# Where the weights lie in their slot, and which half of a k tile comes first: a hybrid RWKV-7 and short convolution block on one core

## The chip, the cores and the metric

The kernel runs on one core of one Trainium2 chip. The metric is the device time of one execution in microseconds (us). Before the change it is 1021.4 us, the median of 3 runs (1020.84 to 1022.16).

## The reference, cut to what matters

One layer over 528 tokens (16 learned ones and 512 of the input), 2048 wide, in float32:

```python
hn = _rmsnorm(h_res, norm_in_g[l])
P = hn @ w_in[l]                       # 2048 -> 65 * 128 columns
Pr, Pc = P[..., :RW_COLS], P[..., RW_COLS:]
prev = jnp.pad(Pr[:, :-1], ((0, 0), (1, 0), (0, 0)))
Pr = Pr + (prev - Pr) * mu_shift[l]
# Pr: r, k, v, g_r (1024 columns each) and two low rank inputs (64 each)
# y = RWKV-7 recurrence of r, decay, k, v, kk, a; 16 heads of 64
y_a = (yn + bonus.reshape(bsz, L, D_RWKV)) * jax.nn.silu(g_r)
# Pc: Bg, Cg, hc, g_c (1024 columns each)
y_b = Bg * _causal_depthwise_conv(Cg * hc, conv_w[l]) * jax.nn.silu(g_c)
h_res = h_res + jnp.concatenate([y_a, y_b], axis=-1) @ w_out[l]
out = _rmsnorm(h_res, norm_f_g)[:, N_META:]
```

What counts here is the first product, `hn @ w_in`: 65 tiles of 128 columns each, which take most of the kernel's time. Everything else is fitted between its matmuls.

## The kernel before, in words

**The projection.** The normalised input lies transposed in SBUF as two parts, xh (the rounded float32r values) and xl (what is left), each of 16 rows (`KT`) of 640 columns (`XROW`, L50), of which 528 are tokens. A tile of the projection is 128 of w_in's columns. Its 2048 by 128 weights come as two transfers of 128 by 1024 (`wr`, three buffers) on SP's queue; each is cut into two quarters of 512 columns, and a quarter is split by ScalarE (the high part, L137) and VectorE or GpSimd (the low part, L138) into a slot `w`. There are six slots in a ring, each 1152 columns wide (`SLOT`) and so 4608 bytes from the next; the high part starts at column `at` of the slot, the low part 512 columns behind it (`slot`, L125). `column` (L115) gives `at` for each tile: 16 for k, v and the low rank inputs (lora), 0 for B and gc, and 8i, 8i + 64, 8i, 8i + 64 for r, g, C, h of index i = 0 to 7. Nothing else depends on `at`. These four lines give 16 different positions.

**The matmuls of a tile** (`steps`, L322, and `main`, L339). A tile is computed for all tokens in one or two pieces, each in its PSUM bank: k, v and lora in pieces of 256 and 272 columns (`FULL`), r, g, C and h in 256 and 258 (`TAIL`), B and gc in one of 512 (`REAL`). Per quarter the pieces come one after the other, the 256 columns first; in a piece the four weight blocks k, and for each block three matmuls: high weights with xh, high weights with xl, low weights with xh. Each matmul has its own weight load. So a tile in two pieces is 4 x 2 x 4 x 3 = 96 matmuls, a quarter 24, a piece of a quarter 12.

```python
for k in ks:
    for n, (ww, xx) in enumerate(((hi, xh), (hi, xl), (lo, xh))):
        nc.tensor.matmul(ps[r], ww[:, w], xx[:, kt, a:b], ...)
```

The change's words count a "distance" from weights to moving columns in bytes, modulo 512.

**Order.** `plan` (L102) lists the tiles: lora, k 0, r 0, B 0 (these four run together over quarters in `mains`, L483), then v 0, k 1, r 1, v 1, g 0, g 1, C 0, h 0, gc 0, and for each further pair of heads k, r, v, k, r, v, g, g, C, h, B, gc; at last C, h, B, gc of 4 to 7. The order of TensorE is written by hand: the projection is a generator of single matmuls, and the other parts of the work call `fill(ns)`, which lets so much of the projection (0.43 ns a column) run between their own matmuls. VectorE, ScalarE, GpSimd and SP are ordered by a scheduler that goes by priorities and expected times, so their order can move when TensorE's does.

**What runs between.** For each pair of heads `prepare` (L628) makes the decay (matmuls tz, ta), the gram matrices (g) and, on VectorE alone, the inverse of small blocks: the blocks go by DMA to sg and come back as d, the result y goes out to sx and comes back as xT. `invert` (L832) then needs xT transposed on VectorE (xn, L845) for the matmuls t (L854). `recur` (L941) runs the recurrence over 9 chunks among the last C, h, B and gc tiles. The finished tiles are read from PSUM by VectorE (`scaled`, L348, line 354 of the profile), in pieces: 256 columns, then the second piece in one or more parts (three for the 272 of k and v). h's result hh goes through GpSimd and ScalarE into cv on VectorE. After the last tile comes the product with w_out (line 1242).

Of the kernel before, what the change touches and what calls it, by code (L numbers as in the profile page):

```python
# [77 lines left out]
def hymba_kernel(ctx: ExitStack, tc: tile.TileContext, xt, xtok, front, w_in, w_out, pv, lup, cst, msk, gf, out):  # L78
# [23 lines left out]
    plan = [("lora", 0), ("k", 0), ("r", 0), ("B", 0), ("v", 0), ("k", 1), ("r", 1), ("v", 1), ("g", 0), ("g", 1)]  # L102
# [10 lines left out]
    N_IN = len(stream)  # L113

    def column(j):  # L115
        what, i = plan[j]
        return {
            "k": 16, "v": 16, "lora": 16, "B": 0, "gc": 0,
            "r": 8 * i, "g": 8 * i + 64, "C": 8 * i, "h": 8 * i + 64,
        }[what]  # L120
    stream += [w_out[0, g] for g in range(3)]
    quarters, chain, low = {}, {}, {}
    state = {"next": 0}
# [5 lines left out]
    def slot_of(q):  # L129
        if q >= 2 * N_IN:  # L130
            return slot(f"w{q}", OUT_AT)
        n = q // 2
        return slot(f"w{q}", column(n % 4 if n < 8 else n // 2))
# [7 lines left out]
    def prefetch(upto):  # L141
        while state["next"] < min(upto, len(stream) if chain else N_IN):
            j = state["next"]
            raw = chain[j - N_IN] if j >= N_IN else wp.tile([P, 1024], F32, tag="raw", name=f"wr{j}", bufs=3)
            state["dma"] = nc.sync.dma_start(raw, stream[j]).ins
            with tc.high_priority(offset=WEIGHTS):
                for q in range(2):
                    split_w(2 * j + q, raw[:, q * 512 : (q + 1) * 512], nc.gpsimd if q and 10 < j < N_IN else nc.vector)
            state["next"] = j + 1
# [172 lines left out]
    def steps(ps, ranges, k4, q, ks=range(4), rs_=range(2)):  # L322
        hi, lo = quarters[q]
        for r, (a, b) in enumerate(ranges):
            if r not in rs_:
                continue
            for k in ks:
                kt = 4 * k4 + k
                w = slice(k * P, (k + 1) * P)
                for n, (ww, xx) in enumerate(((hi, xh), (hi, xl), (lo, xh))):  # L330
                    nc.tensor.matmul(  # L331
                        ps[r], ww[:, w], xx[:, kt, a:b], start=(kt == 0 and n == 0), stop=(kt == KT - 1 and n == 2)
                    )
                    yield (b - a) * 0.43

    def banks(ranges, name, pool, tag):
        return [pool.tile([P, b - a], F32, tag=tag, name=f"ps_{name}_{r}") for r, (a, b) in enumerate(ranges)]

    def main(j, ranges, name):  # L339
        prefetch(2 * j + 4)  # L340
        ps = banks(ranges, name, pm, "main")
        for k4 in range(4):
            if k4 == 1:
                prefetch(2 * j + 5)
            yield from steps(ps, ranges, k4, 4 * j + k4)
        return ps

    def scaled(ranges, ps, dst, base):  # L348
# [134 lines left out]
    def mains():  # L483
# [35 lines left out]
        for j in range(4, len(plan)):  # L519
            what, i = plan[j]  # L520
            rg = FULL if what in ("k", "v") else REAL if what in ("B", "gc") else TAIL
            ps = yield from main(j, rg, f"{what}{i}")
            if what == "B" and i < 4:
                state["split"] = low[4 * j + 4]
            use(what, i, ps)
# [692 lines left out]
    def here(t, n):  # L1218
        return xa[t][:, n * 512 : (n + 1) * 512] if n < 2 else xb[n - 2][:, t]
# [147 lines left out]
    for u, unit in enumerate(units):  # L1367
        half, prod, g = unit
# [53 lines left out]
    with tc.manual_schedule(engines={mybir.EngineType.DVE, mybir.EngineType.Activation, mybir.EngineType.Pool}):  # L1422
# [16 lines left out]
        for part in range(2):  # L1439
# [7 lines left out]
            h = here(1, 2)[:, cols]  # L1447
# [71 lines left out]
```

## Time and profile before

| | |
|---|---|
| median of 3 runs | 1021.4 us |
| the profiled execution | 1022.35 us |
| its span, first to last instruction | 1020.6 us |
| granted TensorE clock, mean over the span | 0.995 |
| tiles of C, h, r, g, k, v (96 matmuls each) without interruption | 11.3 to 11.6 us |
| tiles of B and gc (48 matmuls each) without interruption | 10.9 to 11.4 us |

The page of the profile gives busy time by engine, the chain of work that ended last, and groups of instructions by line; PE is TensorE's matmuls, PEld its weight loads, which overlap them, DVE VectorE, ACT ScalarE, POOL GpSimd, and SP the queue of most DMAs. The view of stretches gives the busy time and number of instructions of each engine between two times. Where its limits are the first matmul of a tile and the first of the next, its length is the time of that tile; an instruction that reaches over a limit is counted too, so the number of matmuls is one or two above 96 there.

### The profile page before, as it was taken

How to read it: one execution, taken by the hardware profiler on the slowest of the kernel's cores; microseconds unless marked ns; L12 is line 12 of the kernel's file. 1: busy time of each engine (PE TensorE's matmuls, PEld its weight loads, DVE VectorE, ACT ScalarE, POOL GpSimd, SP SyncE). 2: the span in 40 equal slices, each digit the busy share in tenths (PEclk: the TensorE clock that was granted, in tenths of full speed). 3: DMA queues.
4: the chain of work that ended last, by engine and by line, in shares of the span. 5: the costliest groups of instructions: out<-in, count | busy, mean ns of one | idle time of the engine just before them, and what ended most of it. 6: DMA issues, size and time to landing. Idle time of an engine off the chain costs nothing.

```text
span 1020.6 us, 23761 instructions
## 1 busy us (share of the span) xinstructions
PE 1001.5 (98%) x9723; PEld 919.9 (90%) x9723; DVE 688.1 (67%) x1305; ACT 393.9 (39%) x729; POOL 274.8 (27%) x292
## 2 busy tenths in 40 slices
PE   9999999999999999999999999999999999999996
PEld 8899998999988999998999998989888897787885
DVE  6677964587765569655568654244555697998787
ACT  7553422344323433322434322222222335545453
POOL 0122323233222323222323222123332333005001
PEclk9999999999999999999999999999999999999999
DMA  9525476446574364864263855977673687695754
GB/s 317 163 69 146 124 197 161 124 119 150 132 191 128 99 165 99 205 179 117 85 167 98 219 141 168 339 248 233 212 215 95 177 270 190 179 321 139 177 127 165
DMA packets 185037, 174.83 MB, mean 171 GB/s; under 512 B 121568, under 2 KB 142816, under 8 KB 184416
## 3 DMA queue, kind: packets, MB, share of 16 engines
q1 hardware_dynamic: 182336, 164.40, 55.0%
q0 software_dynamic: 2304, 8.39, 4.8%
q8 instruction: 76, 1.25, 0.5%
q10 hardware_dynamic: 288, 0.52, 0.1%
q14 instruction: 33, 0.27, 0.1%
HBM read 136.92 MB, written 36.35 MB: 170 GB/s over the span
## 4 chain that ended last, share of the span: by engine, by line
PE 56%; DVE 8%; DMA 3%; issue 3%; ACT 1%; POOL 0%; DVEq 0%; ACTq 0%; SPq 0%; POOLq 0%
PE ps_gc L331 8%; PE ps_B L331 7%; PE ps_h L331 7%; PE ps_C L331 7%; PE ps_v L331 5%; PE ps_g L331 5%; PE ps_k L331 5%; PE ps_r L331 4%; DVE o L1215 3%; DMA wo<-in_w_out_dram 2%; PE M L1242 2%; PE zs L1007 1%; PE zy L1011 1%; PE rz L955 1%; PE g L682 1%
## 5 line engine op out<-in xcount | busy, mean ns | idle before, releaser
L137 ACT CAST w<-wr 128x512 fp32r<-128x512 f32 x252 | 152.8, 618 | 295.4 <-PE ps_k L331 45.0
L138 POOL TENSOR_TENSOR w<-wr,w 128x512 fp32r<-128x512 f32 x119 | 165.4, 1390 | 368.7 <-ACT w L137 317.1
L138 DVE TENSOR_TENSOR w<-wr,w 128x512 fp32r<-128x512 f32 x133 | 96.3, 730 | 105.7 <-ACT w L137 95.7
L331 PE MATMUL ps_k<-xh,w 128*128 128x256 f32 (+1 forms) x512 | 95.9, 284 | 1.1 <-DVE w L138 1.1
L331 PE MATMUL ps_r<-xh,w 128*128 128x256 f32 (+1 forms) x512 | 95.9, 282 | 0.0
L331 PE MATMUL ps_h<-xh,w 128*128 128x258 f32 (+1 forms) x512 | 95.3, 284 | 0.0
L331 PE MATMUL ps_v<-xh,w 128*128 128x272 f32 (+1 forms) x512 | 95.1, 283 | 0.0
L331 PE MATMUL ps_C<-xh,w 128*128 128x258 f32 (+1 forms) x512 | 94.4, 283 | 0.0
L331 PE MATMUL ps_g<-xh,w 128*128 128x258 f32 (+1 forms) x512 | 93.1, 282 | 0.0
L331 PE MATMUL ps_B<-xh,w 128*128 128x512 f32 x256 | 84.3, 398 | 0.0
L331 PEld LDWEIGHTS ps_k<-xh,w 128*128 128x128 f32 x512 | 80.4, 189 | 1.8 <-DVE w L138 1.4
L331 PE MATMUL ps_gc<-xh,w 128*128 128x512 f32 x256 | 81.6, 393 | 0.2 <-DVE w L138 0.2
L331 PEld LDWEIGHTS ps_r<-xh,w 128*128 128x128 f32 x512 | 80.4, 189 | 0.3
L331 PEld LDWEIGHTS ps_h<-xh,w 128*128 128x128 f32 x512 | 80.0, 189 | 0.7
L331 PEld LDWEIGHTS ps_C<-xh,w 128*128 128x128 f32 x512 | 79.9, 189 | 0.6
L331 PEld LDWEIGHTS ps_v<-xh,w 128*128 128x128 f32 x512 | 80.0, 189 | 0.3
L331 PEld LDWEIGHTS ps_g<-xh,w 128*128 128x128 f32 x512 | 79.5, 189 | 0.3
L331 PE MATMUL ps_h<-xl,w 128*128 128x256 f32 (+1 forms) x256 | 72.2, 282 | 0.8 <-issue 0.8
L331 PE MATMUL ps_k<-xl,w 128*128 128x256 f32 (+1 forms) x256 | 72.6, 284 | 0.0
L331 PE MATMUL ps_g<-xl,w 128*128 128x256 f32 (+1 forms) x256 | 72.5, 283 | 0.0
L331 PE MATMUL ps_v<-xl,w 128*128 128x256 f32 (+1 forms) x256 | 72.5, 283 | 0.0
L331 PE MATMUL ps_r<-xl,w 128*128 128x256 f32 (+1 forms) x256 | 72.2, 282 | 0.0
(321 smaller groups left out, 2283.2 us busy)
## 6 DMA issues: line engine op xcount, KB each, us to landing
wr<-in_w_in_dram SPq DMA_DIRECT2D x126, 512.0 KB
ct<-opd SPq DMA_DIRECT2D x64, 288.0 KB
wo<-in_w_out_dram SPq DMA_DIRECT2D x24, 512.0 KB
x<-in_w_out_dram POOLq DMA_DIRECT2D x16, 512.0 KB, 5.7
opd<-ar SPq DMA_DIRECT2D x8, 576.0 KB
opd<-gt SPq DMA_DIRECT2D x16, 288.0 KB
opd<-bt SPq DMA_DIRECT2D x64, 64.0 KB
x<-in_w_out_dram SPq DMA_DIRECT2D x8, 512.0 KB
```

The lines of the kernel that those rows point to most:

```text
L137: nc.scalar.copy(hi, rq)
L138: low[q] = eng.tensor_tensor(out=lo, in0=rq, in1=hi.bitcast(F32), op=ALU.subtract).ins
L331: nc.tensor.matmul(ps[r], ww[:, w], xx[:, kt, a:b], start=(kt == 0 and n == 0), stop=(kt == KT - 1 and n == 2))
L682: nc.tensor.matmul(z[h][:, c - c0], bk[hs, c, h : h + 2, :].rearrange("p a s -> p (a s)"), ar[hs, c].rearrange("p a s -> p (a s)"), start= ...
L955: nc.tensor.matmul(z[e][ho if e else hs, 0, k], t[hs, o : o + CH], t[hs, O_V : O_V + CH] if part else st[hs, 4 * e + k], start=(part == 0 ...
L1007: nc.tensor.matmul(d[hs, j], w, x[hs], start=(a == 0), stop=(a == b - 1))
L1011: nc.tensor.matmul(d[ho, j], t[hs, o : o + CH], x[hs], start=(a == 0), stop=(a == b - 1))
L1215: nc.vector.tensor_tensor(out=lo, in0=rq, in1=hi.bitcast(F32), op=ALU.subtract)
L1242: nc.tensor.matmul(bank[s], left(prod, jj, m, s), w, start=(jj == 0 and n == 0), stop=(jj == 7 and n == 2))
```

## The change

`column` gives one position to k, r, C and lora (16, the default) and one to v, g and h (80), in place of 16 for k, v and lora and of the positions by index for r, g, C and h; B and gc stay at 0. And in the tiles of k that `main` computes (k 1 to k 7) the piece of 272 columns comes before the piece of 256 in each quarter. The number of instructions and the sizes of all buffers stay.

```diff
     def column(j):
-        what, i = plan[j]
-        return {
-            "k": 16, "v": 16, "lora": 16, "B": 0, "gc": 0,
-            "r": 8 * i, "g": 8 * i + 64, "C": 8 * i, "h": 8 * i + 64,
-        }[what]
+        what = plan[j][0]
+        return {"B": 0, "gc": 0, "v": 80, "g": 80, "h": 80}.get(what, 16)
...
         for k4 in range(4):
             if k4 == 1:
                 prefetch(2 * j + 5)
-            yield from steps(ps, ranges, k4, 4 * j + k4)
+            for r in (1, 0) if name[0] == "k" else range(len(ranges)):
+                yield from steps(ps, ranges, k4, 4 * j + k4, rs_=(r,))
         return ps
```

In the scheduler's order of the changed kernel VectorE reads the 272 column piece of k first and the 256 column piece last. A few other instructions change places: in the second pair of heads one transfer `wr` stands ahead of the load of d (d<-sg) on SP's queue, and opd<-ar ahead of the loads of xT; the order around xn there stays.

## The prediction

> **What bounds the kernel now.** I read the page first, then the busy time by stage, then TensorE's list of waits. The span, the busy row and the chain's shares:
>
> ```profile
> span 1020.6 us, 23761 instructions
> PE 1001.5 (98%) x9723; PEld 919.9 (90%) x9723; DVE 688.1 (67%) x1305; ACT 393.9 (39%) x729; POOL 274.8 (27%) x292
> PE 56%; DVE 8%; DMA 3%; issue 3%; ACT 1%; POOL 0%; DVEq 0%; ACTq 0%; SPq 0%; POOLq 0%
> ```
>
> TensorE is busy 98% of the span. The table of stretches says where it isn't (columns: stretch, its length, then busy time and count of PE, PEld, DVE, ACT, POOL, then granted clock, DMA share, GB/s):
>
> ```profile
> 0.00:55.00 55.00, 51.65 (x352) 46.69 (x353) 38.58 (x84) 33.45 (x66) 5.10 (x21) 1.00 0.67 226
> 55.00:329.00 274.00, 270.48 (x2593) 258.41 (x2592) 191.97 (x407) 100.49 (x188) 78.18 (x93) 0.99 0.53 141
> 329.00:479.00 150.00, 150.00 (x1411) 143.47 (x1411) 95.72 (x206) 53.65 (x98) 45.83 (x50) 1.00 0.56 146
> 479.00:629.00 150.00, 150.00 (x1413) 143.51 (x1412) 95.69 (x205) 53.49 (x97) 45.82 (x42) 1.00 0.53 140
> 629.00:853.00 224.00, 223.19 (x3267) 200.24 (x3267) 122.09 (x199) 65.09 (x123) 71.35 (x56) 1.00 0.72 224
> ```
>
> All the tiles of r, C, k, g, h and v but the first k and r lie between 55 and 853 us, and there TensorE rests 274.00 - 270.48 + 224.00 - 223.19 = 4.3 us of 798. So in these stages the end moves with the time that the matmuls themselves take, unless one of the few waits grows. The two longest there are:
>
> ```profile
> engine line waited for: us in total, times, longest us
> PE t L854 <- DVE xn L845: 2.2, 1, 2.2
> PE ps_k L331 <- DVE w L138: 1.1, 1, 1.1
> ```
>
> **The matmuls by distance.** A slot of weights is 4608 bytes apart from the next, a row of the moving x 2560, a weight block 512, and a piece of x starts at byte 0 or 1024: all multiples of 512. So within a tile the distance of weights to moving columns, taken modulo 512 bytes, is one number, 4 x column + 384 (column 16 gives 448, column 80 gives 704 - 512 = 192, as the change has it). Before, r and C of index i stand at 384 + 32i, g and h at 128 + 32i. That makes the old kernel a measurement of its own: equal tiles of 96 matmuls at all 16 distances. Stretches from the first matmul of a tile to the first of the next, where nothing else lies between, give the price of each: C 0, C 1, C 2, C 3, C 4, g 5, C 7 in the first fence (distances 384, 416, 448, 480, 0, 288, 96).
>
> ```profile
> 134.22:145.75 11.54, 11.54 (x98) 11.54 (x97) 5.11 (x20) 3.11 (x5) 2.71 (x4) 1.00 0.86 219
> 275.47:286.92 11.45, 11.45 (x98) 11.45 (x97) 9.46 (x34) 3.11 (x5) 2.71 (x3) 1.00 1.03 282
> 430.19:441.46 11.27, 11.27 (x98) 11.27 (x97) 10.48 (x31) 3.16 (x5) 3.75 (x2) 1.00 0.64 180
> 579.97:591.41 11.44, 11.44 (x98) 11.44 (x97) 10.65 (x31) 3.15 (x5) 3.68 (x2) 1.00 0.61 171
> 629.06:640.61 11.55, 11.55 (x97) 11.55 (x96) 4.41 (x6) 3.12 (x5) 2.59 (x2) 1.00 0.84 276
> 418.69:430.19 11.50, 11.50 (x98) 11.50 (x97) 4.99 (x15) 3.63 (x6) 2.69 (x4) 1.00 0.91 219
> 808.19:819.55 11.36, 11.36 (x97) 11.36 (x96) 10.57 (x16) 5.14 (x10) 2.82 (x2) 1.00 0.78 223
> ```
>
> And h 0 and h 1 (128 and 160):
>
> ```profile
> 145.75:157.30 11.55, 11.55 (x98) 11.55 (x97) 7.65 (x24) 1.15 (x2) 1.30 (x1) 1.00 0.91 233
> 286.92:298.37 11.44, 11.44 (x98) 11.44 (x97) 6.92 (x11) 1.25 (x2) 1.29 (x1) 1.00 0.67 169
> ```
>
> Two things are to be seen. A tile at 448 takes 11.27 us, the others 11.36 to 11.55, though PEld is busy in every one from end to end. And h agrees with C to 0.01 us at a distance 256 higher, so 192 should be worth what 448 is. It isn't the other engines: DVE is busier beside C 2 (10.48 us) than beside C 0 (5.11), and DMA share 1.03 beside C 1 goes with a shorter tile than 0.86 beside C 0.
>
> The Trainium skill speaks against this change. "TensorE: Matmul & The Clock Gate", section "Step-by-step: what each phase is for", says that the moving operand and the weight load have independent SBUF read ports, so that loading the next weights takes nothing from the running matmul; by that rule no column would matter and the time would stay 1021.4 us. The rows above do not agree with it: 0.28 us of 11.55 hang on the column.
>
> **r, C, g and h, term by term.** No instruction is added or removed; a slot is 1152 columns wide whatever column is used. Against 11.27 each index saves: 0: 11.54 - 11.27 = 0.27; 1: 0.18; 2: 0; 3: 0.17; 4: 0.28; 5: 0.23; 7: 0.09. Index 6 (64, 320) is always interrupted; its last quarter of r 6 against one quarter of C 2:
>
> ```profile
> 499.98:502.82 2.84, 2.84 (x26) 2.84 (x25) 1.77 (x5) 2.81 (x7) 1.70 (x2) 1.00 0.19 30
> 435.83:438.65 2.81, 2.81 (x26) 2.81 (x25) 2.61 (x7) 0.62 (x1) 1.86 (x1) 1.00 0.48 80
> ```
>
> 0.03 a quarter, 0.12 a tile. That is 1.34 us for eight tiles, 5.4 us for the four kinds. I leave out r 0's 0.27: it lies in the first 55 us, of which TensorE works 51.65, and there the inputs set the time. 5.1 us stay.
>
> From it I take what the entry costs. Pieces of twelve 256 column matmuls at 448: inside C 2, inside k 4, the first of r 2 (behind a k), the second of r 2, the first of v 7 (behind an r):
>
> ```profile
> 433.02:434.39 1.37, 1.37 (x14) 1.37 (x13) 1.13 (x8) 0.62 (x1) 0.00 (x0) 1.00 1.01 351
> 331.50:332.91 1.41, 1.41 (x14) 1.41 (x13) 1.21 (x2) 0.62 (x1) 0.00 (x0) 1.00 0.00 0
> 184.19:185.60 1.41, 1.41 (x14) 1.41 (x13) 1.32 (x4) 0.62 (x1) 0.46 (x1) 1.00 0.00 0
> 187.05:188.43 1.38, 1.38 (x14) 1.38 (x13) 0.58 (x4) 0.88 (x2) 0.00 (x0) 1.00 0.59 145
> 541.87:543.24 1.37, 1.37 (x14) 1.37 (x13) 1.34 (x2) 0.04 (x1) 0.00 (x0) 1.00 0.78 158
> ```
>
> At one and the same distance there are two paces: 1.37 or 1.38 behind a piece of 258 columns, 1.41 behind one of 272. So the first piece of r 1 to 7 (behind k), of g 0, 2, 4, 6 (behind v) and, I assume, of C 4 to 7 (behind gc) runs at the slow pace: 15 pieces by 0.04 = 0.6 us. The sum is 5.1 - 0.6 = **4.5 us**; its bounds are 5.4 (no slow entry, r 0 counted) and 2.5 (the second rival).
>
> **v at 192.** C and h show no difference between distances 256 apart, so I take 0, the nearest rows. From both sides: its three slow pieces of 256 columns in four, if they went fast, give 24 by 0.04 = 1.0 us off; a fall to the dearest row, 0.28 a tile, would be 2.2 us on.
>
> **The 272 columns first in k.** The matmuls and their weights are the same, and the turn from 272 to 256 columns, behind which the pace is slow, comes as often: inside a quarter now, between quarters before. Whole tiles of k 4 and v 5 at 448:
>
> ```profile
> 328.60:340.18 11.59, 11.59 (x97) 11.58 (x96) 4.54 (x8) 3.12 (x5) 2.58 (x2) 1.00 0.59 165
> 391.90:403.45 11.55, 11.55 (x98) 11.55 (x97) 10.59 (x16) 2.81 (x5) 2.96 (x3) 1.00 0.45 112
> ```
>
> I take 0 again. Bounds: 7 tiles by 4 pieces by 0.04 = 1.1 us off if the turn inside a quarter leaves the fast pace; 0.04 a tile, 0.3 us on, if it costs a piece more. The evacuation of k now ends with one 256 column product on VectorE in place of three for the 272; k's consumers are not among TensorE's waits.
>
> **Do the waits eat it?** The wait of 1.1 us is behind VectorE's read of gc's bank, which waits for TensorE itself, and the one of 2.2 us for xn closes a chain that starts at TensorE's h 1:
>
> ```profile
> 168.93 0.69 DVE L354 TENSOR_TENSOR gc<-ps_gc,rs 128x512 f32<-128x512 f32 x1 [5.38 <-PE ps_gc L331]
> 298.91 0.15 DVE L354 TENSOR_TENSOR hh<-ps_h,rs 128x2 f32<-128x2 f32 x1
> 301.23 1.54 DVE L431 SCALAR_TENSOR_TENSOR cv<-u,pvt,cv 128x512 f32<-128x512 f32 x2 [2.17 <-ACT cv L429]
> 302.69 3.45 DVE L138 TENSOR_TENSOR w<-wr,w 128x512 fp32r<-128x512 f32 x2
> 306.06 0.70 DVE L845 STREAM_TRANSPOSE xn<-xT 128x512 f32<-128x512 f32 x1
> 306.81:310.30 3.49, 3.49 (x38) 2.89 (x39) 0.69 (x1) 2.11 (x4) 0.12 (x1) 0.51 0.69 222
> ```
>
> The stretch from h 1's end to xn holds only B 1's matmuls, which stay as they are; so both waits, and the 3.49 us at clock 0.51 that follow the second, move earlier with TensorE and keep their size. I put the loss at 0.
>
> The profiled execution took 1022.35 us, 1.75 around its span of 1020.6, and stands 0.95 above the median of 1021.4. 1022.35 - 4.5 = 1017.85 beside it; beside the median **1016.9 us**.
>
> **Rivals.**
> *The 256 column pieces of k and v go fast as well* (1.1 and 1.0 us): 1016.9 - 2.1 = 1014.8. For it: the pace depends on what went before, and the change alters that for k. Against: the turn from 272 to 256 is still there. 0.15.
> *The 256 column pieces of r and g all stay slow*, since r stands behind k and g behind v: 15 tiles by 4 pieces, less the 11 charged already, 49 by 0.04 = 2.0 us: 1018.9. For it: the first piece of r 2 is slow. Against: its second is not, 1.38. 0.1.
> *The distance isn't the cause*: weight loads and moving columns don't meet, something else made the tiles differ, and the change does nothing: 1021.4. It is what the Trainium skill's rule on the read ports gives. Against: C 0 and h 0, C 1 and h 1 agree, and C 2 stands alone at 11.27 between C 1 and C 3, 150 us to either side. 0.1.
> *Slower:* in the changed order one weight transfer stands ahead of d<-sg on SP's queue in the second pair.
>
> ```profile
> 275.07 0.30 SPq L622 DMA_DIRECT2D d<-sg  x1
> 275.47 1.33 SPq L145 DMA_DIRECT2D wr<-in_w_in_dram  x1
> 290.73 0.68 DVE L790 TENSOR_REDUCE y<-prod 72x64 f32<-72x512 f32 x1
> 294.88 0.44 SPq L805 DMA_DIRECT2D sx<-y  x1
> SPq L145 <- DVE w L138: 163.3, 56, 8.9
> ```
>
> SP waits up to 8.9 us for a buffer before such a transfer; d, the inverse y and xn behind it would be as late. y is ready at 291.41 and goes out at 294.88, so 3.5 us of that are free and 8.9 - 3.5 = 5.4 would be new idle time: 1016.9 + 5.4 = 1022.3. It decides from 4.5 + 3.5 = 8.0 us on. Against: in the old order that transfer took only 1.33 us. 0.05.
>
> **Chances.** The forecast has 0.6. About 0.2% (2 us) is what a measurement can tell from no change. Faster by more (under 1019.4): 0.6 + 0.15 + 0.1 = 0.85. Within: 0.1 and most of the slower rival, 0.13. Slower by more: 0.02. The range takes in the first three cases and, at the top, waits grown by 3 us: 1014.0 to 1020.0.
>
> **What would show it.** Tiles of C, h, r, g that all last 11.25 to 11.35 us where nothing interrupts them, B and gc as before; pieces of 1.37 us inside them; k and v near 11.59 and 11.55; the same three waits. Wrong it would be if a C or h tile at 448 or 192 still took 11.4 or more, or if a new wait of over 2 us stood between 55 and 853 us.

## The result and the profile after

| | before | after |
|---|---|---|
| median | 1021.42 us (1020.84 to 1022.16, 6 runs) | 1017.45 us (1016.34 to 1019.25, 6 runs) |
| the profiled execution, its span | 1022.35, 1020.6 us | 1016.83, 1015.1 us |

The ratio of after to before is 0.9963, with a 95% interval of 0.995 to 0.9976: 4 us faster, the interval from 2.5 to 5.1 us of 1021.4. The prediction said 1016.9 us.

The page of the changed kernel: span and busy row.

```profile
span 1015.1 us, 23761 instructions
PE 995.6 (98%) x9723; PEld 913.6 (90%) x9723; DVE 684.3 (67%) x1305; ACT 393.9 (39%) x729; POOL 276.2 (27%) x292
```

The number of instructions is the same, and TensorE is busy 5.9 us less. Most of that lies in the tiles of r, C, g and h, and 1.6 us of it in B 1, which comes below. Stretches of the changed kernel for the same seven tiles as before (C 0, C 1, C 2, C 3, C 4, g 5, C 7), columns as before:

```profile
133.46:144.71 11.25, 11.25 (x98) 11.25 (x97) 4.07 (x18) 2.50 (x4) 2.79 (x4) 1.00 0.83 207
274.17:285.42 11.25, 11.25 (x98) 11.25 (x97) 8.68 (x33) 3.12 (x5) 2.57 (x2) 1.00 0.92 225
426.05:437.31 11.25, 11.25 (x98) 11.25 (x97) 10.47 (x31) 3.15 (x5) 3.75 (x2) 1.00 0.68 185
575.69:586.95 11.25, 11.25 (x98) 11.25 (x97) 10.46 (x31) 3.15 (x5) 3.74 (x2) 1.00 0.65 183
624.40:635.71 11.30, 11.30 (x97) 11.30 (x96) 4.37 (x6) 3.12 (x5) 2.57 (x2) 1.00 0.84 276
414.80:426.05 11.25, 11.25 (x98) 11.25 (x97) 5.00 (x15) 3.63 (x6) 2.69 (x4) 1.00 0.91 220
802.50:813.80 11.30, 11.30 (x97) 11.30 (x96) 10.83 (x17) 4.87 (x9) 2.66 (x2) 1.00 0.75 221
```

Where before they took 11.27 to 11.55 us, they now take 11.25, and 11.30 where the tile follows gc (C 4, C 7). h 0 and h 1, k 4 and v 5:

```profile
144.71:155.96 11.25, 11.25 (x98) 11.25 (x97) 8.75 (x25) 1.77 (x3) 1.28 (x1) 1.00 0.97 253
285.42:296.68 11.26, 11.26 (x98) 11.26 (x97) 6.86 (x12) 1.26 (x2) 1.97 (x1) 1.00 0.60 144
325.14:336.76 11.62, 11.62 (x97) 11.62 (x96) 4.69 (x10) 3.12 (x5) 2.59 (x2) 1.00 0.60 165
388.23:399.76 11.53, 11.53 (x98) 11.53 (x97) 10.57 (x16) 2.80 (x5) 2.95 (x3) 1.00 0.47 112
```

k 4 takes 0.04 us more than before (11.585 to 11.622 us), v 5 0.02 less. Pieces of 256 columns inside C 2, inside k 4, and the second of r 2:

```profile
428.87:430.24 1.37, 1.37 (x14) 1.37 (x13) 1.13 (x8) 0.62 (x1) 0.00 (x0) 1.00 1.11 325
329.56:330.97 1.41, 1.41 (x14) 1.41 (x13) 0.10 (x1) 0.00 (x0) 0.00 (x0) 1.00 0.90 264
185.87:187.25 1.38, 1.38 (x14) 1.38 (x13) 0.57 (x5) 0.85 (x2) 0.00 (x0) 1.00 0.49 95
```

The two paces at one distance are still there. TensorE's waits in the projection:

```profile
engine line waited for: us in total, times, longest us
PE t L852 <- DVE xn L843: 2.0, 1, 2.0
PE ps_k L328 <- DVE w L135: 1.1, 1, 1.1
```

They kept their size. What did not stay is what followed the wait for xn. B 1, in which it lies, in the kernel before and in the changed one:

```profile
298.37:315.87 17.51, 15.34 (x178) 12.21 (x177) 9.62 (x15) 5.53 (x10) 6.06 (x5) 0.90 0.55 156
```

```profile
296.68:312.42 15.74, 13.77 (x178) 11.00 (x177) 9.42 (x15) 5.53 (x10) 6.07 (x5) 1.00 0.61 173
```

Clock 0.90 before, 1.00 after, and 1.77 us less: in this execution the wait of 2.0 us was not followed by the half clock. So the two profiled executions are 5.5 us apart, where the medians are 4.0 apart.

### The profile page after: what moved, and what is told of

Same layout as the page of the kernel before. It is cut to its first block, busy times and chain, and to the rows that moved or that the text cites. A ratio compares the mean times of both kernels' runs of the same rounds, so it can differ in the third digit from the quotient of the medians.

```text
span 1015.1 us, 23761 instructions
## 1 busy us (share of the span) xinstructions
PE 995.6 (98%) x9723; PEld 913.6 (90%) x9723; DVE 684.3 (67%) x1305; ACT 393.9 (39%) x729; POOL 276.2 (27%) x292
## 4 chain that ended last, share of the span: by engine, by line
PE 55%; DVE 8%; DMA 3%; issue 2%; ACT 1%; SPq 0%; POOL 0%; DVEq 0%; ACTq 0%; POOLq 0%
PE ps_gc L328 8%; PE ps_B L328 7%; PE ps_h L328 7%; PE ps_C L328 6%; PE ps_v L328 5%; PE ps_k L328 5%; PE ps_g L328 4%; PE ps_r L328 4%; DVE o L1213 3%; DMA wo<-in_w_out_dram 2%; PE M L1240 2%; PE zy L1009 1%; PE zs L1005 1%; PE g L680 1%; DVE xb L1221 1%
## 5 line engine op out<-in xcount | busy, mean ns | idle before, releaser
L328 PE MATMUL ps_k<-xl,w 128*128 128x272 f32 (+1 forms) x256 | 73.1, 286 | 0.0
```

The costliest lines, as they stand in the source:

```text
L328: nc.tensor.matmul(ps[r], ww[:, w], xx[:, kt, a:b], start=(kt == 0 and n == 0), stop=(kt == KT - 1 and n == 2))
```

## The experiments

My theory: the pace of a tile is set by the distance of weights to moving columns, modulo 256 bytes, and on top of it by the width of the piece that ran just ahead; the columns carry the whole gain and the order of k brings nothing. Rivals: the order carries a part; the place of the weights counts and not the distance; the distance is not the cause. Times are medians; each ratio is to runs of the kernel before on the same chip.

**The columns without the order.**

```diff
-            for r in (1, 0) if name[0] == "k" else range(len(ranges)):
-                yield from steps(ps, ranges, k4, 4 * j + k4, rs_=(r,))
+            yield from steps(ps, ranges, k4, 4 * j + k4)
```

> The change without the order: columns 16 and 80, and k again with its 256 columns first. Theory (the columns carry all of it): the median stays within 0.5 us of the changed kernel's 1017.5, uninterrupted tiles of C, h and odd g last 11.25 us, k 4 goes back from 11.62 to 11.59 us. Rival (the order carries a part): the gain of 4 us shrinks by 1 us or more.

Measured: 1017.8 us, ratio 0.9957 (0.9944 to 0.9969), against 0.9963 (0.995 to 0.9976) with the order. C 0 and k 4:

```profile
133.25:144.50 11.25, 11.25 (x98) 11.25 (x97) 4.08 (x18) 3.11 (x5) 2.69 (x4) 1.00 0.86 220
324.87:336.45 11.58, 11.58 (x97) 11.58 (x96) 4.53 (x8) 3.12 (x5) 2.56 (x2) 1.00 0.59 166
```

The whole gain is there without the order, and k 4 is back at 11.58.

**The order without the columns**: the old `column`, the new loop over the pieces of k.

> The order without the columns: the 16 old distances, k with its 272 columns first. Theory: no gain, 1021.4 us within 0.5; C 0 lasts 11.54 us as before and k 4 11.62. Rival (the order carries a part): 1 us or more below 1021.4, and pieces of 256 columns in k at 1.37 us.

Measured: 1021.37 us, ratio 0.9995 (0.9986 to 1.0004). C 0 and k 4:

```profile
134.35:145.90 11.54, 11.54 (x98) 11.54 (x97) 4.21 (x19) 3.11 (x5) 2.81 (x4) 1.00 0.86 210
327.17:338.80 11.63, 11.63 (x97) 11.62 (x96) 4.67 (x10) 3.11 (x5) 2.59 (x2) 1.00 0.60 165
```

No difference that can be measured, and k 4 pays its 0.04 us. The rival of the order falls.

**All of r, C, g and h at the dearest distance.**

```diff
-        return {"B": 0, "gc": 0, "v": 80, "g": 80, "h": 80}.get(what, 16)
+        return {"B": 0, "gc": 0, "v": 80, "g": 96, "h": 96, "r": 32, "C": 32}.get(what, 16)
```

> The changed kernel with r and C at column 32 (distance 0) and g and h at column 96 (256), the dearest of the 16; v and k as changed. Theory (distance sets the pace): every uninterrupted r, C, g and h tile lasts 11.5 to 11.55 us; against before, where seven of eight indices are cheaper, 8 x 0.28 - 1.34 = 0.9 us a kind, 3.6 us for four, so about 1025 us, 7 to 8 us above the changed kernel. Rival (weight loads and moving columns do not meet, and something beside the tiles made them differ): 1017 to 1021 us, tiles spread as before.

Measured: 1024.67 us, ratio 1.0027 (1.0016 to 1.0038). C 1, C 2 and C 7:

```profile
276.04:287.52 11.48, 11.48 (x98) 11.48 (x97) 8.85 (x33) 3.11 (x5) 2.57 (x2) 1.00 0.92 237
430.80:442.34 11.55, 11.55 (x98) 11.55 (x97) 10.76 (x31) 3.13 (x5) 3.59 (x2) 1.00 0.65 176
810.66:822.21 11.55, 11.55 (x97) 11.55 (x96) 10.44 (x16) 5.20 (x10) 3.12 (x2) 1.00 0.78 231
```

C 2 has moved from 11.27 to 11.55 us at the same place in the program, and C 3, C 4 and C 7 are there too: nearly all of the spread of the old kernel was the distance, not what runs beside a tile. A rest of 0.07 us is not explained by it: C 1 and h 1 stand at the same distances and take 11.48 us.

**Distance or place: the moving columns moved, then both.** First x alone goes 64 bytes up, then the weights follow it.

```diff
-    xh = xp.tile([P, KT, XROW], F32R, name="xh")
-    xl = xp.tile([P, KT, XROW], F32R, name="xl")
+    xh = xp.tile([P, KT, XROW], F32R, name="xh")[:, :, 16 : 16 + L]
+    xl = xp.tile([P, KT, XROW], F32R, name="xl")[:, :, 16 : 16 + L]
```

```diff
-        return {"B": 0, "gc": 0, "v": 80, "g": 80, "h": 80}.get(what, 16)
+        return {"B": 16, "gc": 16, "v": 96, "g": 96, "h": 96}.get(what, 32)
```

> The changed kernel with the moving x (xh and xl) 16 columns, 64 bytes, further in its rows; the weights stay where the change put them. Theory (it is the distance of weights to moving columns that counts): every distance falls by 64, r, C, g and h stand at 384 and 128 and last 11.54 us where nothing interrupts them, 31 tiles by about 0.27 = 8.4 us on; k and v pay 0.2 us a tile by the scan, 3 us, B and gc up to 0.1 us, 1.5 us: 1029 to 1030 us. Rival (the place of the weights alone counts): 1017.5 us, C tiles at 11.25.

> The same with the weights of all tiles moved 16 columns as well: the distances are those of the changed kernel again, the places are not. Theory: 1017.5 us within 1, C tiles at 11.25 us. Rival (the place counts, of the weights or of x): 1 us or more off.

Measured: with x alone 1028.85 us, ratio 1.0067 (1.0053 to 1.0081); with both 1018.31 us, ratio 0.9964 (0.995 to 0.9978). C 2 and v 5, x alone:

```profile
432.08:443.62 11.55, 11.55 (x98) 11.55 (x97) 10.76 (x31) 3.14 (x5) 3.60 (x2) 1.00 0.66 177
393.59:405.33 11.74, 11.74 (x98) 11.74 (x97) 10.74 (x17) 2.65 (x5) 3.06 (x4) 1.00 0.42 107
```

and with the weights moved after it:

```profile
427.41:438.66 11.25, 11.25 (x98) 11.25 (x97) 10.46 (x31) 3.15 (x5) 3.75 (x2) 1.00 0.65 182
389.52:401.05 11.53, 11.53 (x98) 11.53 (x97) 10.57 (x16) 2.82 (x5) 2.96 (x3) 1.00 0.46 112
```

With the weights untouched the tiles slow down; with everything moved the tiles that nothing cuts are back to 0.02 us. The distance decides, the place does not. The Trainium skill's rule, in "TensorE: Matmul & The Clock Gate", section "Step-by-step: what each phase is for", that loading weights takes nothing from the running matmul since the two have read ports of their own, does not hold as it stands here: by it 64 bytes could not cost the 10.5 us between these two kernels. What collides inside the chip, no run shows.

**The scan for the other widths.** k, v (256 and 272 columns), B and gc (512) at all distances, r, C, g, h as changed.

```diff
-        what = plan[j][0]
-        return {"B": 0, "gc": 0, "v": 80, "g": 80, "h": 80}.get(what, 16)
+        what, i = plan[j]
+        return {"B": 8 * i, "gc": 8 * i + 64, "k": 8 * i, "v": 8 * i + 64, "g": 80, "h": 80}.get(what, 16)
```

> The changed kernel with the tiles that were never scanned at all distances: k at column 8i, v at 8i + 64, B at 8i, gc at 8i + 64 (i = 0 to 7), so the old scan now for pieces of 256 and 272 columns and of 512. Theory (the distance modulo 256 sets the pace, for every width): k and v spread by 0.1 to 0.3 us a tile with the least at i = 2 (448, 192), B and gc spread too and tell whether 384 (i = 0) is their dearest place. Rival (only pieces of 256 and 258 columns are touched): all within 0.05 us of the changed kernel's k, v, B and gc.

Measured: 1023.15 us, one run. k 4 (distance 0), v 5 (288), v 7 (352), B 7 (96), gc 6 (320) and gc 7 (352):

```profile
327.77:339.56 11.78, 11.78 (x97) 11.78 (x96) 4.67 (x10) 3.12 (x5) 2.57 (x2) 1.00 0.59 163
391.51:403.27 11.76, 11.76 (x98) 11.76 (x97) 10.77 (x17) 2.80 (x5) 2.94 (x3) 1.00 0.45 110
542.20:553.84 11.65, 11.65 (x98) 11.65 (x97) 10.64 (x16) 2.60 (x4) 3.75 (x3) 1.00 0.46 110
831.25:842.45 11.20, 11.20 (x50) 9.01 (x49) 10.85 (x17) 4.63 (x10) 3.49 (x3) 1.00 0.77 259
797.70:808.69 10.99, 10.99 (x49) 9.02 (x48) 4.06 (x6) 4.70 (x8) 3.85 (x3) 1.00 0.86 237
842.45:853.64 11.20, 11.20 (x49) 9.00 (x48) 6.15 (x9) 2.81 (x5) 6.04 (x4) 1.00 0.74 194
```

B 7 and gc 7 of the changed kernel, at 384:

```profile
825.05:835.96 10.91, 10.91 (x50) 9.02 (x49) 10.56 (x17) 4.34 (x9) 3.49 (x3) 1.00 0.84 268
835.96:846.84 10.88, 10.88 (x49) 9.01 (x48) 6.51 (x9) 3.10 (x6) 6.02 (x4) 1.00 0.86 210
```

Every width is touched, and 448 and 192 are the best place for k and v too: there they take 11.62 and 11.53 us. The tiles that other matmuls cut say the same, each against its own time in the changed kernel: the nearest to it is v 3 at 224, 0.03 us dearer, and the farthest v 0 at 128, 0.31. But for 512 columns the cheapest of the scanned places is 384, where B and gc stand already, one at which 256 and 258 columns are dear (11.54 us, C 0 before). The tiles of B and gc at other places are 0.08 to 0.32 us dearer than in the changed kernel (B 1, which has the half clock, left out). My expectation left open which place is best for this width.

**The pace and the width ahead.** C's second piece made 272 columns wide, the 14 more not read.

```diff
-            rg = FULL if what in ("k", "v") else REAL if what in ("B", "gc") else TAIL
+            rg = FULL if what in ("k", "v", "C") else REAL if what in ("B", "gc") else TAIL
```

> The changed kernel with the second piece of every C tile 272 columns wide in place of 258 (the 14 more are not read), distance and all else the same. Theory (the width of the piece ahead sets the pace of a 256 column piece): the 256 column pieces of C go from 1.37 to 1.41 us in all quarters but the first, the 272 column ones last 1.48, a whole tile 11.53 to 11.58 us as v does, 8 x 0.3 = 2.4 us on in all. Rival (the pace belongs to k and v, by their place in the order): the 256 column pieces of C stay at 1.37, a tile lasts 11.25 + 4 x 0.04 = 11.4 us.

Measured: 1018.37 us beside 1020.58 for the kernel before, one run each; these totals can't show 2 us, the tiles can. In C 2, the 256 and the 272 columns of the second quarter and the whole tile:

```profile
429.40:430.82 1.41, 1.41 (x14) 1.41 (x13) 1.18 (x8) 0.62 (x1) 0.00 (x0) 1.00 1.22 296
430.82:432.30 1.48, 1.48 (x14) 1.48 (x13) 1.27 (x7) 0.00 (x0) 0.00 (x0) 1.00 0.87 285
426.55:438.08 11.53, 11.53 (x98) 11.53 (x97) 10.74 (x31) 3.15 (x5) 3.62 (x2) 1.00 0.68 181
```

C now goes as v does: 1.41 behind 272 columns in place of 1.37 behind 258, at the same distance and with matmuls of the same size. The pace goes on into the next tile: h 0, behind C 0, takes 11.32 us here and 11.25 in the changed kernel.

**k, v and lora in two halves of 264 columns.**

```diff
-    FULL = ((0, HALF), (HALF, L))
+    FULL = ((0, L // 2), (L // 2, L))
```

> The changed kernel with k, v and lora in two pieces of 264 columns in place of 256 and 272. The second piece then starts 1056 bytes in, so its distance is 32 lower than the first's: 448 and 416 for k, 192 and 160 for v. Theory (width and distance both count): the slow 256 pieces go, but the second piece pays about half of the 0.18 us between C 2 and C 1: a k tile between 11.5 and 11.7 us, the kernel within 1 us of 1017.5. Rival (272 columns alone are dear): k and v at 11.4 us or less, 2 us off.

Measured: 1018.51 us, one run; k 4 takes 11.655 us and v 5 as much (from first matmul to first matmul), where the changed kernel has 11.62 and 11.53. In one quarter of v 5, the half at 192 and the half 32 bytes lower:

```profile
391.95:393.42 1.47, 1.47 (x14) 1.47 (x13) 1.47 (x3) 0.92 (x2) 0.00 (x0) 1.00 0.17 33
393.42:394.86 1.45, 1.45 (x14) 1.45 (x13) 1.32 (x3) 0.37 (x2) 0.97 (x1) 1.00 0.00 0
```

Nothing is won, but not as I expected: the half that stands 32 bytes off is the cheaper one. Why the half at the best distance is dear with 264 columns stays open.

**The wait for xn taken away**: 4 us more of the projection ahead of the second pair's t, on the changed kernel, and on the columns alone.

```diff
-        fill(FW["solve"] if first else FW["solve_first"])
+        fill((FW["solve"] + 4000 * (first == 2)) if first else FW["solve_first"])
```

> The changed kernel with 4 us more of the projection ahead of the second pair's matmuls t. Theory (the wait for xn of 2 us is what the change left in the projection, and the half clock of 3.4 us behind it comes in some executions only and makes the spread): the wait is gone, 2 us off, and the upper runs near 1019 lose 1.7 us more: 1015 to 1015.5 us, with less spread. Rival (what follows t is as tight): the wait comes back at xm or at a split of weights, 1017 us or above.

> The columns of the change, k with its 256 columns first as before, and the 4 us more ahead of t. Theory (the order of k costs 0.04 us in k 4, 5, 6 and 7 and as much in v 2 and v 3, some 0.25 us in all, and brings nothing): 0.2 to 0.3 us below e7_solve_later, which the runs may not separate but the tiles do (k 4 at 11.58 us). Rival (the order pays elsewhere): 0.3 us or more above it.

Measured: 1015.05 us (1014.48 to 1016.0), ratio 0.9934 (0.992 to 0.9948); and with the columns alone 1014.75 us (1013.04 to 1015.62), ratio 0.9927 (0.9914 to 0.9939). TensorE's longest waits in the first of them:

```profile
engine line waited for: us in total, times, longest us
PE prs L475 <- POOL yb L468: 1.7, 1, 1.7
PE M L1240 <- ACT o L1212: 1.5, 1, 1.5
PE pwarm L187 <- DVE cold L184: 1.4, 1, 1.4
PE ps_k L328 <- DVE w L135: 1.1, 1, 1.1
```

t is not among them any more, and the wait hasn't come back elsewhere. The second kernel has the lowest median here. That it is below the first can't be told: the intervals overlap.

## Why the prediction was right, point by point

- *TensorE's own matmuls set the end between 55 and 853 us.* Right: the tiles' saving is the kernel's.
- *The distance sets the price, 11.27 us at 448 and 192.* Right, 11.25, and shown by moving x alone and both. The 384 of the prediction's formula stands in no view; nothing rests on it, since the runs compare differences of distance alone.
- *The sum of 4.5 us.* The total came out, but one term was wrong in size. Tile by tile (first matmul to the next tile's first, before less after, added over the tiles of a kind) h saves 1.38 us, 0.12 of it shorter waits, g 1.34 and C 1.19, where the prediction has 1.34, 1.18 and 1.18. But r 1 to 7 save only 0.34 of the 0.79 that it counts. In all 4.25 for 4.5; less the 0.23 that k and the 0.08 that v lose, 3.9; the medians are 4.0 apart. r is the term that was mis-sized. r 6 and r 7, cut four times each by the small matmuls tz and ta, went from 12.30 and 12.34 us to 12.36 each. They gained nothing: the prices of 0.12 and 0.09 came from tiles or quarters that nothing cuts. In r 6, nine matmuls of 256 columns behind two of 272 in ta, then the 256 and the 258 columns of the last quarter, which nothing cuts; before:

```profile
497.26:498.32 1.06, 1.06 (x11) 1.06 (x10) 1.06 (x1) 0.00 (x0) 0.00 (x0) 1.00 0.00 0
499.98:501.39 1.42, 1.42 (x14) 1.42 (x13) 0.35 (x2) 1.42 (x5) 1.25 (x1) 1.00 0.06 12
501.39:502.82 1.43, 1.43 (x14) 1.43 (x13) 1.43 (x4) 1.40 (x4) 0.45 (x1) 1.00 0.31 49
```

  and after:

```profile
493.20:494.26 1.06, 1.06 (x11) 1.06 (x10) 1.06 (x1) 0.00 (x0) 0.00 (x0) 1.00 0.00 0
495.94:497.32 1.37, 1.37 (x14) 1.37 (x13) 0.30 (x2) 1.37 (x5) 1.20 (x1) 1.00 0.06 12
497.32:498.76 1.44, 1.44 (x14) 1.44 (x13) 1.44 (x4) 1.41 (x4) 0.47 (x1) 1.00 0.26 71
```

  In r 6 the pieces of 258 columns gain nothing at 448, so all has to come from those of 256, and of these the ones behind a wide matmul of ta stay at the slow pace, 0.117 us each and not 0.114. The prediction priced the slow pace for the first piece of a tile alone. Another 0.1 of r's shortfall comes with the order of k: with the columns alone r saves 0.45. The interval of the total, 2.5 to 5.1 us, could not have told 4.5 from 4.0; that r was too high shows in the tiles alone.
- *The first piece behind k, v and gc is slow, 0.04 us each.* Right (C 4 and C 7 pay 0.05, g 0 0.06), and for 272 columns the run with the wide C shows that the width of the piece ahead makes it so; the 512 of gc were not varied.
- *v at 192 and the order of k: 0.* Within the bounds given, but not 0: k 1 to 7 take 0.23 us more and v 0.08. With the columns alone k is where it was and v 0.06 cheaper, so it is the order that costs this.
- *The waits keep their size, the half clock behind the second too.* The waits did. The half clock did not: of the ten profiles here that have this wait (1.8 to 2.6 us), four show clock 0.5 for 3.4 us behind it (before, the dearest distance, the scan, both moved) and six do not; the last section has what sets them apart. Runs of one kernel seem to differ in it too: of the six runs of the changed kernel the two with the lowest mean clock, 0.996, took 1019.07 and 1019.25 us, the other four at most 1017.79.
- The rivals: that the 256 column pieces of r stay slow came true for a part, in r 3 to r 7 behind tz and ta; the others did not. The transfer ahead of d<-sg held nothing up; the wait for xn at the end of that chain was no longer than before.

## What to carry to other kernels

Where weights are loaded for every matmul, treat the distance in SBUF between the weights and the moving columns as something to tune: try it over 256 bytes, for each width of the moving operand by itself, since the best place for 512 columns was a dear one for 256. A kernel that gives each of its equal tiles another distance measures all of them in one profile. And when TensorE sets the end, look for the last waits of 2 us: one of them here was worth 2.4 us in the medians, more than half of what all the distances were.

## What the runs showed of the hardware that I had not expected

- The effect goes with the distance modulo 256 bytes: C at 448 and h at 192 both take 11.25 us, C 7 and h 7 both 11.55 (11.550 and 11.545) at 0 and 256.
- It is small and has no good value of its own: 11.25 against 11.55 us for 96 matmuls of 256 and 258 columns, 3 ns a matmul; 11.53 against 11.76 for 256 and 272; 10.88 against 11.20 for 48 of 512.
- At one distance a row of 256 column matmuls goes at either of two paces, 1.37 or 1.41 us for twelve, and stays in the one that the piece ahead leaves it in: 258 columns the faster, 272 the slower.
- A wait of 2 us can halve the clock for 3.4 us, and where it falls decides. In each of the twelve traces the clock changes only at borders that lie whole numbers of 3.413 us apart, in the kernel before at 6.52, 306.89, 310.30, 863.26, 866.67 and 1016.86 us. In the four profiles with the half clock the whole wait for xn lies between two borders; in the other six a border divides it. In the kernel before, the stretch between two borders that holds the wait, and the next one:

```profile
303.48:306.89 3.41, 1.25 (x39) 0.76 (x41) 3.28 (x3) 0.00 (x0) 2.36 (x3) 1.00 0.45 145
306.89:310.30 3.41, 3.41 (x38) 2.81 (x39) 0.69 (x1) 2.11 (x4) 0.12 (x1) 0.50 0.67 214
```

  In the changed kernel, the two stretches that share the wait:

```profile
300.57:303.98 3.41, 2.59 (x41) 1.86 (x39) 3.41 (x3) 1.01 (x2) 3.32 (x3) 1.00 0.46 151
303.98:307.40 3.41, 2.27 (x39) 1.94 (x40) 1.09 (x2) 1.54 (x4) 0.17 (x1) 1.00 0.77 233
```

  Over all the stretches at full clock in the twelve traces, the clock was halved behind every one in which TensorE was busy for 1.68 us or less and behind none with 1.70 or more, about half of 3.41. The Trainium skill, "TensorE: Matmul & The Clock Gate", section "What's actually happening", ties the clock to free-running windows of 3.4 us. The borders agree: the first of them falls between 4.3 and 7.2 us from one profile to the next. The same section of the Trainium skill lets the clock fall after an idle window of about 3.4 us. The traces differ: a stretch with 1.68 us of work was enough.
